# A two-layer hybrid encoder in split float32: 1/rms moved from the tokens to the evictions, and layer 0 started from feature-major tokens

## The chip, the cores and the metric

One core of a Trainium2 chip runs the whole kernel. The metric is the device time of one execution in microseconds; smaller is better. The engines are named as the profile names them: PE (TensorE), PEld (its weight loads), DVE (VectorE), ACT (ScalarE), POOL (GpSimd), SP (SyncE, which here only issues transfers).

## What is computed

512 tokens of 2048 features pass two layers. Per layer, cut to what matters here:

```python
h = rmsnorm(x, g_pre)                       # x * rsqrt(mean(x*x) + EPS) * g_pre
z = h @ w_in                                # columns: GLA q,k,v,gate, low-rank forget gate, attention q,k,v,gate
log_a = log_sigmoid(ga @ w_alpha + b_alpha) / 16
o_gla = rmsnorm(gla_chunk_causal(gq, gk, gv, log_a), g_gla) * silu(gg)
scores = einsum(aq, ak) * D ** -0.5 + rel_bias[clipped distance]     # -inf where masked
o_att = rmsnorm(softmax(scores) @ av, g_att) * silu(ag)
y = concat([o_gla, o_att]) @ w_out
x = x + rmsnorm(y, g_post)
```

`1/rms` is one number a token. A product is linear in its tokens, so the factor can be applied to the tokens before a product or to its result.

## The kernel before, in words

**Precision.** Every float32 operand is split into a high part (a cast on ACT) and a remainder (a subtraction on DVE). A product is three matmuls: high x high, high x low, low x high. Weights come in chunks of 256 rows of a block of 512 columns (512 KB): `raw` or `H` is the chunk, `wh` its high part (L183, ACT), `wl` its remainder (L187, DVE). A token operand `a` is [128, 2 parts, 512]: two slices of 128 features for a half of the tokens (256).

**Blocks.** A layer's input projection has 14 blocks of 512 columns. The first two, the gates of attention, are plain products: `std_gemm` (L283) goes over 8 chunks of features in the order `CO`, for each over its token tiles (128 tokens, four in all), with 6 matmuls a tile and chunk. Each tile has a PSUM bank of its own (four banks for products in all, `ps_mm`, four for other work, `ps_ax`). The very first block is run twice, over token tiles 0 and 1, then 2 and 3, and its weights are loaded and split twice. The other twelve are paired; a pair is one Strassen-like product with seven parts P1 to P7 (`fast_gemm`, L357, or L347 where the result is wanted feature-major). Some operands of these parts are sums of token halves (`token_sums`: S1 to S4, stored to DRAM and read back as `sa`). Results are completed at eviction: a finished sum is kept by `copies` (L314, ACT) and joined with PSUM by `combine` (L319, DVE). The output projection is two plain blocks and one pair (`W23`).

**The start.** `prep_half` prepares half the tokens: load rows (token-major), sum of squares (`square_sum`, L416 on ACT, L417 on DVE), 1/rms by a power on POOL (`rsqrt`, L403), scale the rows (L456, DVE), and for each of 8 chunks four transposes on PE (L466), a scale by the feature gain `gcol` (L476, ACT) and the split (L105 ACT, L106 DVE). In layer 1 the rows come from `finish_token` (the residual sum, L1113, DVE), which also stores them to `x_mid`.

**Users of the products.** Gates go through SiLU (L583) to DRAM. Keys and queries are split per head; queries take the factor -QS, the bias is negated on ACT (L709), and one DVE instruction (L734) adds bias to the scores and gives their minimum, from which ACT takes exp(-x) (L738). The forget gate is a narrow product (L605, 64 matmuls) beside the second block.

**Order.** Engine queues run in order. Main products and side work are interleaved by hand: side work is a list of generators (`tasks`), and `pump` takes some steps after each group of matmuls (`rate`); `until(cond)` takes steps till a condition on the program's own state holds; `drain` takes all. Weight jobs are prepared up to five ahead (`ahead`: loads 5, high parts 4, remainders 3). From the instructions in that order a planner with a cost model makes the order of each engine's queue: what its model sees ready earlier can go earlier. `issue_after` keeps an instruction behind another one on its engine. SP's queue holds the weight loads, the `sa` loads and small loads such as the bias; POOL's holds the stores.

## Time and profile before

| | |
|---|---|
| median of 3 runs | 1702.46 us (1696.93 to 1706.23) |
| profiled execution, span from first to last instruction | 1701.1 us; the page gives no other time of this execution |
| busy: PE / PEld / DVE / ACT / POOL | 1648.9 / 1403.5 / 1209.9 / 873.2 / 160.0 us |
| mean granted clock of PE | 0.991 |
| moved by DMA | 455.04 MB, mean 268 GB/s |

Busy times of engines overlap. A matmul's own length (mean 0.39 us for 512 columns) is longer than the distance at which they follow each other, since they are pipelined. Times in a timeline count from the start of the span; "[1.8 <-X]" behind a row says how long its engine had stood idle and what ended that.

### The profile page before, as it was taken

What the parts mean: (1) busy time and instruction counts of PE and PEld (TensorE: products, weight loads), DVE (VectorE), ACT (ScalarE), POOL (GpSimd) and SP (SyncE); (2) the same over time, 40 slices, a digit from 0 to 9 for tenths busy, and PEclk for the clock granted to TensorE, in tenths of its full rate; (3) what the DMA queues carried; (4) which work ended last, traced back from release to release, by engine and by line L of the source; (5) the groups of instructions that cost most, each with busy time, mean ns of one, the idle gap of its engine ahead of it and who ended that gap; (6) DMA issues with size and microseconds to landing.
All of it is one profiled execution on the core that took longest, in us unless ns stands there. A gap on an engine that the chain in (4) does not pass through costs nothing. (4 is left out here: it accounts for less than half of the span.)

```text
span 1701.1 us, 24915 instructions
## 1 busy us (share of the span) xinstructions
PE 1648.9 (97%) x9090; PEld 1403.5 (83%) x9090; DVE 1209.9 (71%) x1563; ACT 873.2 (51%) x1460; POOL 160.0 (9%) x256
## 2 busy tenths in 40 slices
PE   7999999999999999999999999999999999999995
PEld 5888878999987877787778878799999888777884
DVE  5846867686776876468887567668777667854886
ACT  8634544455665544345684345345556555433443
POOL 0210000001000101210122000000001001022101
PEclk8999999999999999999999999999999999999998
DMA  7986877868858797589779688868587678865993
GB/s 259 364 301 226 331 255 265 281 203 273 294 184 279 242 348 252 175 315 314 251 239 370 240 294 297 290 233 291 192 298 256 210 259 268 300 232 197 354 334 135
DMA packets 143002, 455.04 MB, mean 268 GB/s; under 512 B 15444, under 2 KB 32212, under 8 KB 142880
## 3 DMA queue, kind: packets, MB, share of 16 engines
q1 hardware_dynamic: 119984, 373.76, 64.2%
q0 software_dynamic: 22176, 78.41, 11.9%
q8 instruction: 72, 1.18, 0.3%
q10 hardware_dynamic: 720, 1.28, 0.2%
q14 instruction: 50, 0.41, 0.1%
HBM read 381.28 MB, written 72.11 MB: 267 GB/s over the span
## 5 line engine op out<-in xcount | busy, mean ns | idle before, releaser
L357 PE MATMUL mm<-wh,sa 128*128 128x512 f32 x1536 | 490.3, 394 | 9.1 <-ACT wh L183 4.0
L183 ACT CAST wh<-raw 128x1024 fp32r<-128x1024 f32 x248 | 261.8, 1057 | 276.8 <-PE mm L357 76.4
L187 DVE TENSOR_TENSOR wl<-raw,wh 128x1024 fp32r<-128x1024 f32 x248 | 301.8, 1221 | 96.5 <-PE mm L283 32.2
L357 PEld LDWEIGHTS mm<-wh,sa 128*128 128x128 f32 x1536 | 289.7, 189 | 74.5 <-ACT wh L183 5.8
L183 ACT CAST wh<-H 128x1024 fp32r<-128x1024 f32 x224 | 234.8, 1052 | 225.2 <-PE mm L357 123.9
L187 DVE TENSOR_TENSOR wl<-H,wh 128x1024 fp32r<-128x1024 f32 x224 | 272.3, 1221 | 93.8 <-PE mm L357 33.5
L357 PE MATMUL mm<-wl,sa 128*128 128x512 f32 x768 | 303.2, 395 | 9.5 <-DVE wl L187 9.4
L347 PE MATMUL mm<-sa,wh 128*128 128x256 f32 x1280 | 236.9, 285 | 0.0
L347 PEld LDWEIGHTS mm<-sa,wh 128*128 128x128 f32 x1280 | 200.2, 191 | 0.4
L357 PE MATMUL mm<-wh,a 128*128 128x512 f32 x576 | 184.0, 393 | 2.6 <-DVE t L319 2.6
L347 PE MATMUL mm<-sa,wl 128*128 128x256 f32 x640 | 181.3, 283 | 0.0
L357 PEld LDWEIGHTS mm<-wl,sa 128*128 128x128 f32 x768 | 145.4, 189 | 43.5 <-DVE wl L187 14.5
L283 PE MATMUL mm<-wh,a 128*128 128x512 f32 x512 | 169.4, 395 | 3.6 <-ACT a L105 1.8
L176 DVE TENSOR_TENSOR H<-H,raw 128x1024 f32<-128x1024 f32 x112 | 136.7, 1222 | 1.9
L357 PEld LDWEIGHTS mm<-wh,a 128*128 128x128 f32 x576 | 107.3, 188 | 25.1 <-DVE t L319 3.0
L347 PEld LDWEIGHTS mm<-sa,wl 128*128 128x128 f32 x640 | 122.5, 191 | 0.0
L180 DVE TENSOR_TENSOR raw<-H,raw 128x1024 f32<-128x1024 f32 x48 | 58.8, 1225 | 86.1 <-DMA raw<-in_w_dram 86.0
L403 POOL TENSOR_TENSOR sm<-sm,mhalf 128x2 f32<-128x2 f32 (+2 forms) x44 | 53.2, 1210 | 688.6 <-DVE sm L777 459.9
L283 PEld LDWEIGHTS mm<-wh,a 128*128 128x128 f32 x512 | 95.9, 188 | 26.0 <-ACT a L105 2.3
L357 PE MATMUL mm<-wl,a 128*128 128x512 f32 x288 | 113.5, 394 | 0.9 <-DVE wl L187 0.9
L283 PE MATMUL mm<-wl,a 128*128 128x512 f32 x256 | 100.5, 393 | 0.5 <-DVE wl L187 0.4
L347 PE MATMUL mm<-a,wh 128*128 128x256 f32 x512 | 94.8, 284 | 0.0
(193 smaller groups left out, 2350.9 us busy)
## 6 DMA issues: line engine op xcount, KB each, us to landing
raw<-in_w_dram SPq DMA_DIRECT2D x312, 512.0 KB, 5.2
sa<-S SPq DMA_DIRECT2D x192, 512.0 KB, 5.1
H<-in_w_dram SPq DMA_DIRECT2D x56, 512.0 KB, 4.8
sa<-A SPq DMA_DIRECT2D x48, 512.0 KB, 6.0
S<-g POOLq DMA_DIRECT2D x32, 512.0 KB, 7.8
oS<-g POOLq DMA_DIRECT2D x32, 512.0 KB, 7.1
sa<-oS SPq DMA_DIRECT2D x32, 512.0 KB, 5.5
sg<-t POOLq DMA_DIRECT2D x32, 256.0 KB, 5.5
```

The lines of the kernel that those rows point to most:

```text
L176: nc.vector.tensor_tensor(out=h, in0=h, in1=r, op=ALU.add)
L180: nc.vector.tensor_tensor(out=r, in0=h, in1=r, op=ALU.subtract)
L183: last_cast[0] = nc.scalar.copy(self.wh, src).ins
L187: nc.vector.tensor_tensor(out=self.wl, in0=self.src, in1=self.wh.bitcast(F32), op=ALU.subtract)
L283: nc.tensor.matmul(pss[o], a[:, part, t], rhs[:, kk, :], start=(i == 0 and kk == 0 and m == 0), stop=(i == n - 1 and kk == 1 and m == 2),)
L347: nc.tensor.matmul(dst, lhs[:, kk, f], a[:, part, tok], start=(fresh and kk == 0 and m == 0 and ft % 2 == 0), stop=(c == 3 and kk == 1 and ...
L357: nc.tensor.matmul(out_ps[t], a[:, part, tok], rhs[:, kk, :], start=(fresh and kk == 0 and m == 0), stop=(c == 3 and kk == 1 and m == 2), ...
L403: nc.gpsimd.tensor_tensor(out=out_r, in0=v, in1=mhalf[:, : v.shape[-1]], op=ALU.pow)
```

## The change

Products now take the tokens with only the feature gain applied. 1/rms (and its negative, and rms) of each token is kept in a small tile `norm`, worked out after the operands are prepared (`token_norms`), and also written to DRAM (`r_d`) to be read back as a row across partitions (`norm_row`).

- Evictions multiply by the token's 1/rms: SiLU's scale, `copies`, `combine`, the splits of v, the decay product of k, av. The products of attention's q and k are left as they are: k is multiplied by a row of 1/rms (one more DVE instruction and one small load), and q's factor is applied at the scores, where the bias is first multiplied by rms (one ACT copy a head and tile) and the DVE instruction scales by -1/rms. The bias is no longer negated on load.
- The forget gate's result is multiplied by the row of 1/rms as it leaves PSUM.
- In layer 0 the host gives a second, feature-major copy of the tokens, `xt` (two halves x 8 chunks of 256 KB). Each weight chunk of the first block is loaded between the two halves of its columns; there are no transposes; the gain is applied in place, one 256-wide part on ACT, one on DVE. The rows follow behind the weight chunks 8 to 11, for the squares alone.
- In layer 0 the first block runs once, over all four token tiles.

```diff
 stream: for l in range(L):
-        stream += [Job(l, "std", c, AG0) for c in CO]
-        stream += [Job(l, "std", c, AG0) for c in CO]
+        for _ in range(min(l, 1) + 1):
+            stream += [Job(l, "std", c, AG0) for c in CO]
 Job.load:
-                self.raw = self.fetch(rtile("raw"), b0, c)
+                i = done["load"]
+                if i < NCH:
+                    load_columns(i, 0)
+                    self.raw = self.fetch(rtile("raw"), b0, c)
+                    load_columns(i, 1)
+                else:
+                    self.raw = self.fetch(rtile("raw"), b0, c)
+                if NCH - 1 <= i < NCH + 3:
+                    half, j = divmod(i - NCH + 1, 2)
+                    with tc.issue_after(last_load[0]):
+                        rows[half, j] = load_row(half, j, x, nc.sync)
 copies:
-                nc.scalar.copy(e, src[t])
+                if scaled:
+                    nc.scalar.activation(e, src[t], AF.Copy, scale=inv_rms(l, 2 * (name == "p5") + t))
 combine:
-                nc.vector.tensor_tensor(out=dst, in0=a, in1=b, op=op)
+                if scaled:
+                    r = (inv_rms if sign > 0 else neg_inv_rms)(l, 2 * h + t)
+                    nc.vector.scalar_tensor_tensor(out=dst, in0=ps, scalar=r, in1=kept, op0=ALU.mult, op1=op)
...
+    def token_norms(l, half, xs):
+        cols = slice(2 * half, 2 * half + 2)
+        ss = sm(2)
         for j in range(2):
             square_sum(ss[:, j : j + 1], xs[j])
             yield
+        r = norm[l][:, 0, cols]
         rsqrt(r, ss)
+        nc.vector.tensor_scalar(out=norm[l][:, 1, cols], in0=r, scalar1=-1.0, scalar2=None, op0=ALU.mult)
+        nc.vector.tensor_tensor(out=norm[l][:, 2, cols], in0=ss, in1=r, op=ALU.mult)
         for j in range(2):
-            for z in xs[j]:
-                nc.vector.tensor_scalar(out=z, in0=z, scalar1=r[:, j : j + 1], scalar2=None, op0=ALU.mult)
-            yield
+            t = 2 * half + j
+            nc.gpsimd.dma_start(r_d[l][t * P : (t + 1) * P, :], inv_rms(l, t))
+        normed.add((l, half))
+        yield
+
+    def norm_row(l, tok, n):
+        z = t2((tok.stop - tok.start,))
+        nc.sync.dma_start(z[0:n], r_d[l][tok, :].rearrange("s o -> o s").partition_broadcast(n))
+        return z
 prep_chunk:
+            if l:
+                nc.scalar.activation(d, ps[:, kk * 256 : (kk + 1) * 256], AF.Copy, scale=g)
+            elif kk:
+                nc.vector.tensor_scalar(out=d, in0=d, scalar1=g, scalar2=None, op0=ALU.mult)
+            else:
+                nc.scalar.activation(d, d, AF.Copy, scale=g)
...
+    def prep_half(l, half, xs):
+        for ch in CO:
+            yield from prep_chunk(l, half, ch, xs)
+        yield from token_norms(l, half, xs)
+
+    def prep_first():
+        for i, ch in enumerate(CO):
+            while i not in columns:
+                yield
+            for half in range(2):
+                yield from prep_chunk(0, half, ch, None)
+        for half in range(2):
+            while (half, 1) not in rows:
+                yield
+            yield from token_norms(0, half, [rows[half, j] for j in range(2)])
...
-    xs_first = load_tokens(0, x, nc.sync)
-    prepare("load", 2)
-    xs_second = load_tokens(1, x, nc.sync)
+    prepare("load", 4)
 gate_evac:
-                gate(half, q, o, ps)
+                until(lambda: (l, o // 2) in normed)
+                gate(half, q, o, ps, inv_rms(l, o))
 layer 0, first block:
+            std_gemm(l, AG0, range(NT), CO, operand_in, gate_evac(1, 0), rate=1.0, lag=2)
 Head.scores:
+                nc.scalar.activation(pr, biases[self.hd][:, 512 - lk : 512], AF.Copy, scale=rms(l, i))
                 nc.vector.tensor_tensor_reduce(
-                    out=pr, in0=ps[:, :lk], in1=biases[self.hd][:, 512 - lk : 512], op0=ALU.add, op1=ALU.min,
-                    scale=1.0, scalar=-NEG, accum_out=nmx,
+                    out=pr, in0=ps[:, :lk], in1=pr, op0=ALU.add, op1=ALU.min,
+                    scale=neg_inv_rms(l, i), scalar=-NEG, accum_out=nmx,
 qk_consume, keys:
+                    nc.vector.tensor_tensor(
+                        out=z, in0=z, in1=norm_row(l, hs, P).unsqueeze(1).to_broadcast([P, 2, 256]), op=ALU.mult
+                    )
```

More of the change, by code (lines that the diff above doesn't have):

```diff
@@ L99, in hybrid_trunk @@
     fac_d = [dram([P, 1024], f"fac{l}") for l in range(L)]
+    r_d = [dram([S, 1], f"r{l}") for l in range(L)]
     def flat(t):
@@ L446, in hybrid_trunk, with full_tile, load_columns, inv_rms @@
     full = {}
-    def prep_half(l, half, xs):
-        ss, r = sm(2), sm(2)
+    columns = set()
+    def full_tile(half, c):
+        return rtile("H") if half == 0 else slot(KEEP[c], [2, 512])
+    def load_columns(i, half):
+        kh, c = divmod(CO[i], 4)
+        if kh == 0:
+            full[half, c] = full_tile(half, c)
+        with tc.issue_after(last_load[0]) if last_load[0] else nullcontext():
+            last_load[0] = nc.sync.dma_start(full[half, c][:, kh, :], xt[half, CO[i]]).ins
+        columns.add(i)
+    norm = [small.tile([P, 3, NT], F32, tag="norm", name=nm("norm"), bufs=2) for _ in range(L)]
+    normed = set()
+    def inv_rms(l, t):
+        return norm[l][:, 0, t : t + 1]
+    def neg_inv_rms(l, t):
+        return norm[l][:, 1, t : t + 1]
+    def rms(l, t):
+        return norm[l][:, 2, t : t + 1]
+    def token_norms(l, half, xs):
+        cols = slice(2 * half, 2 * half + 2)
+        ss = sm(2)
         for j in range(2):
@@ L469, in prep_half @@
             if kh == 0:
-                while half == 0 and l and done["low"] < min(h_end + c, len(stream)):
+                h_end = next(i for i, z in enumerate(stream) if z.l == l - 1 and z.b0 == W23[0] and z.kind == "P4")
+                while half == 0 and done["low"] < min(h_end + 1 + c, len(stream)):
                     yield
-                full[half, c] = rtile("H") if half == 0 else slot(KEEP[c], [2, 512])
-            dst = full[half, c][:, kh, :]
-            for kk in range(2):
-                kt = 2 * ch + kk
-                nc.scalar.activation(
-                    dst[:, kk * 256 : (kk + 1) * 256], ps[:, kk * 256 : (kk + 1) * 256], AF.Copy,
-                    scale=gcol[:, base + kt : base + kt + 1],
-                )
@@ L480, in prep_half @@
[L480 to L490 removed]
+                full[half, c] = full_tile(half, c)
+        dst = full[half, c][:, kh, :]
@@ L1149, in w_consume @@
                     pass
-        fast_gemm(l, W23, w_consume, rate=3, end=True, lag=3 if last else 0)
+        fast_gemm(l, W23, w_consume, rate=3, end=True, lag=3 if last else 0, scaled=False)
         for c in range(4):
```

146 lines of the change are left out of this document (87 added, 59 removed).

## The prediction, made before the change was run

> **What bounds the kernel now.** I read the page's head and its slices first, then the stretches in which the slices fall short, then the order of time in those stretches.
>
> ```profile
> span 1701.1 us, 24915 instructions
> PE 1648.9 (97%) x9090; PEld 1403.5 (83%) x9090; DVE 1209.9 (71%) x1563; ACT 873.2 (51%) x1460; POOL 160.0 (9%) x256
> ...
> 0.00:120.11 120.11, 109.50 (x523) 89.81 (x524) 72.61 (x103) 75.34 (x130) 17.73 (x44) 0.96 0.84 312
> 5.20:12.50 7.30, 0.00 (x0) 0.00 (x0) 1.33 (x5) 5.78 (x10) 0.80 (x3) 0.68 1.00 392
> 12.50:18.03 5.53, 5.33 (x25) 4.87 (x25) 4.48 (x7) 4.98 (x11) 0.00 (x0) 0.50 1.04 401
> 18.03:32.00 13.97, 12.14 (x65) 9.66 (x63) 8.68 (x15) 13.97 (x32) 1.23 (x2) 1.00 0.44 161
> 32.00:120.11 88.11, 88.11 (x428) 73.99 (x428) 57.84 (x78) 47.73 (x79) 15.21 (x28) 1.00 0.90 331
> 272.00:460.00 188.00, 188.00 (x1536) 186.19 (x1535) 141.46 (x205) 103.12 (x189) 9.11 (x12) 1.00 0.75 251
> 826.00:890.50 64.50, 58.09 (x275) 46.64 (x274) 54.18 (x76) 54.49 (x107) 16.18 (x29) 0.95 0.67 225
> ```
>
> Columns of the stretches: length, busy time of PE, PEld, DVE, ACT, POOL, granted clock, DMA share, GB/s. TensorE is the bound: 97% busy, and in most stretches without a gap (88.11 of 88.11, 188.00 of 188.00). So only three things move the time: work taken off PE, PE's gaps, and its half clock. Its gaps lie where this change works: in the start (to 120.11, when the first product of the next stage, L357, begins) and at the passage from layer 0 to layer 1 (826 to 890.5, 6.4 us idle and a clock of 0.95). The attention products (272 to 460) have none to give.
>
> The start, in order of time (start, length, engine):
>
> ```profile
> 0.76 0.40 ACTq L534 DMA_DIRECT2D gcol<-in_g_cols_dram  x1
> 4.88 1.06 ACT L416 ACTIVATE t<-g 128x1024 bf16<-128x1024 f32 x1 [1.58 <-DMA g<-in_x_dram]
> 5.84 0.19 ACT L416 ACTIVATION_READ_ACCUMULATOR t<-g 128x1 f32 x1
> 6.54 1.06 ACT L416 ACTIVATE t<-g 128x1024 bf16<-128x1024 f32 x1 [0.51 <-DMA g<-in_x_dram]
> 10.96 0.71 POOL L403 TENSOR_TENSOR sm<-sm,mhalf 128x2 f32<-128x2 f32 x1 [9.94 <-DVE sm L417]
> 11.71 2.74 DVE L456 TENSOR_SCALAR g<-g,sm 128x1024 f32<-128x1024 f32 x4 [0.83 <-POOL sm L403]
> 13.18 5.13 PE L466 MATMUL ax<-cst,g 128*128 128x128 f32 x23 [0.19 <-DVE g L456]
> 18.03 0.52 PE L283 MATMUL mm<-wh,a 128*128 128x512 f32 x1
> 20.44 0.69 ACT L416 ACTIVATE t<-bias 128x512 bf16<-128x512 f32 x1
> 23.73 0.50 PE L283 MATMUL mm<-wh,a 128*128 128x512 f32 x1 [1.76 <-ACT a L105]
> 31.33 0.33 SPq L708 DMA_DIRECT2D bias<-in_rel_dram  x1
> 91.81 2.05 PE L605 MATMUL ax<-g,g 128*96 128x256 f32 x16
> 120.11 0.39 PE L357 MATMUL mm<-wh,a 128*128 128x512 f32 x1
> 1567.15 37.94 PE mm L283 x166
> ```
>
> Tokens land, are squared, rooted on POOL, scaled, transposed, scaled again and split: the first real product is at 18.03, the second group waits for ACT at 23.73, and PE is gapless only from 32. The last row is the price of a 512-wide product in a gapless run: 37.94/166 = 0.2286 us. A forget-gate product is 2.05/16 = 0.128 us, a transpose 5.13/23 = 0.22 at half clock, so 0.11 at full.
>
> **The change, part by part.**
>
> *The start.* Useful PE work before 120.11: 384 products of the first two blocks (192 each, the same number before and after) x 0.2286 = 87.8, and 64 forget-gate products x 0.128 = 8.2: 96.0 us. The rest, 120.1 - 96.0 = 24.1 us, is transposes, idle time and half clock. The change removes the 64 transposes and the chain in front of the first product. What the new first product waits for:
>
> ```profile
> gcol<-in_g_cols_dram ACTq DMA_DIRECT2D x1, 32.0 KB, 4.3
> bias<-in_rel_dram SPq DMA_DIRECT2D x16, 256.0 KB, 4.5
> L183 ACT CAST wh<-raw 128x1024 fp32r<-128x1024 f32 x248 | 261.8, 1057 | 276.8 <-PE mm L357 76.4 <-PE mm L283 50.4 <-DMA raw<-in_w_dram 50.4
> L187 DVE TENSOR_TENSOR wl<-raw,wh 128x1024 fp32r<-128x1024 f32 x248 | 301.8, 1221 | 96.5 <-PE mm L283 32.2 <-PE mm L357 28.0 <-PE mm L347 13.8
> L105 ACT CAST a<-H 128x512 fp32r<-128x512 f32 x16 | 10.0, 675 | 0.0
> L106 DVE TENSOR_TENSOR a<-H,a 128x512 fp32r<-128x512 f32 x16 | 10.7, 687 | 4.8 <-ACT a L105 4.7
> L476 ACT ACTIVATE H<-ax,gcol 128x256 f32<-128x256 f32 x32 | 13.0, 515 | 0.3 <-PE ax L466 0.3
> L709 ACT ACTIVATE bias<-bias 128x512 f32<-128x512 f32 x16 | 10.5, 657 | 18.2 <-DMA bias<-in_rel_dram 18.2
> L456 DVE TENSOR_SCALAR g<-g,sm 128x1024 f32<-128x1024 f32 x12 | 8.6, 750 | 3.2 <-POOL sm L403 3.2
> ```
>
> SP now issues half a chunk of columns (256 KB), the weights (512 KB), the other half. By the rows at 4.88 and 6.54, 512 KB lands at 4.9 and the next 1.66 later, so the columns land near 4.1 and the weights near 5.7 (estimates from those rows). The gains of the features are issued at 0.8 and take 4.3: 5.1, so they come last. Then scale 0.5 (ACT one part, DVE the other) to 5.6, cast 0.68 to 6.3, weight cast 1.06 to 7.35 (the first product), weight remainder 1.22 to 8.6 (the second product, before which PE can't go on). I take 8.6 as the start.
>
> The clock: 0.68 over 5.20 to 12.50 means half clock for 64% of 7.3, that is from 7.8 on, so the first products meet it. Two rows price the way back:
>
> ```profile
> 830.69:834.72 4.03, 4.03 (x10) 2.91 (x10) 3.69 (x5) 2.75 (x5) 1.23 (x3) 0.60 0.96 315
> ```
>
> There a clock of 0.60 over 4.03 us of products is 3.2 us at half speed, 1.6 us lost. At 12.50 to 18.03, 25 matmuls, nearly all transposes, stayed at 0.50 for 5.5 us: 2.8 lost. The new stage begins with products, so I take 1.6 and keep 2.8 as the far end; below stands 0, if the first product comes before 7.8.
>
> The Trainium skill, TensorE: Matmul & The Clock Gate, Part 4, says that transposes don't count as busy for the clock gate, and Part 1 that some 3.4 us of activity release it. The trace agrees so far: 3.2 us of products against 5.5 us of transposes. If the rule did not hold, the far price would go into the sum and the forecast be 1.2 us later.
>
> Supply of the first block: PE needs 24 x 0.2286 = 5.5 us a chunk. ACT has 2 x (0.5 + 0.68) + 1.06 = 3.4, DVE 2 x (0.4 + 0.69) + 1.22 = 3.4 (a 256-wide scale bounded by half of the 0.75 of L456). Into the same eight chunks fall the squares of the four rows, 6 pieces x 1.25 (4.88 with its read at 5.84) and 4 x 0.9 (20.44, with a read) = 11.1 us of ACT: 38.5 of 43.9 us. That is tight, and before, ACT was full (13.97 of 13.97) just where PE waited 1.8 us for it. I put 2.0 us of PE waits here; ends 0 and 4.8 (all gaps and half clock of before between 12.5 and 32: 0.2 + 2.8 + 1.8). The second weight pass goes (8 transfers, 8 casts, 8 remainders); the 4 MB of columns take its place on the queue, and the DMA share of 0.90 stays below one.
>
> Sum: 8.6 + 1.6 + 96.0 + 2.0 = 108.2 against 120.1: **11.9 us** gained. Norms: the rows arrive behind weight chunks 8 to 11, near 40 us by PE's pace of 5.5 us a chunk, and the first eviction is at 10.2 + 156 x 0.2286 = 46; the root is due then, with some 4 us in hand. If late, the next block's first tile still has 3 tiles x 12 products = 8 us before it needs the bank.
>
> *The passage to layer 1.* There the squares, root and scaling leave the way from the residual sum to the transposes:
>
> ```profile
> 868.92 1.41 DVE L1113 SCALAR_TENSOR_TENSOR sg<-g,sm,sg 128x512 f32<-128x512 f32 x2
> 873.95 1.80 POOL L403 TENSOR_TENSOR sm<-sm,mhalf 128x2 f32<-128x2 f32 x1 [2.79 <-DVE sm L417]
> 875.79 1.42 DVE L456 TENSOR_SCALAR g<-g,sm 128x1024 f32<-128x1024 f32 x2 [0.61 <-POOL sm L403]
> 877.35 0.52 PE L466 MATMUL ax<-cst,g 128*128 128x128 f32 x3 [0.36 <-DVE g L456]
> 881.15 0.33 PE L466 MATMUL ax<-cst,g 128*128 128x128 f32 x1 [1.82 <-ACT g L476]
> 884.35 0.78 PE L283 MATMUL mm<-wh,g 128*128 128x512 f32 x1
> ```
>
> Tokens are final at 870.3, transposes start at 877.35: 7 us that the change takes out. The products of the first pass end at 876.8 and those of the second start at 884.35: 7.6 us, of which 32 transposes x 0.11 = 3.5 stay. So at most 4.1 us come back, by the operands' being ready 6 to 7 us sooner. The squares (about 5 us of ACT a half) move behind the preparation, into a stretch where ACT is 54.49 of 64.50 busy; what is late next is ACT's casts, worth some tenths. I take **4.0**; ends 1 and 6 (6.4 idle in the whole stretch; the finishing sums on DVE stay).
>
> *Evictions.* Scaling by a column replaces copies and differences one for one (same shapes, same engines): nothing, PE being covered by 188.00 of 188.00.
>
> *Bias and key rows.* 64 more ACT copies, four a head, of 512, 384, 256 and 128 elements; the first at 0.66, the rest in proportion plus a fixed part, together about 1.8 a head, less one 0.66: +18.7 us on ACT in both layers. 16 key multiplications of 0.69 on DVE: 11 us. Beside 188 us of PE a layer, ACT goes from 103 to 112 and DVE from 141 to 147: hidden. Each multiplication also waits for a small transfer on SP, and behind it on DVE stand the weight remainders:
>
> ```profile
> SPq L166 <- PE mm L347: 99.4, 46, 8.5
> ```
>
> SP waits 2.2 us on average for a buffer (8.5 at worst), and the nearest transfer takes 4.5 (the bias): 6.7 us until it lands. PE then still has two prepared jobs, 24 products each; at 188.00/1536 = 0.122 us that is 5.9. I take 0.12 us of loss each, **2 us** in all; ends 0 and 16 x 0.8 = 13.
>
> *Rest.* One table load fewer, and 8 tiny stores of 1/rms on POOL's queue (beside 160 us of POOL work): nothing.
>
> **Sum:** 1701.1 - 11.9 - 4.0 + 2.0 = 1687.2. The page gives the span alone; the median of the runs shown stands 1.4 above it (1696.93 to 1706.23), so 1688.6, given as **1689 us**, 0.8% faster. About 0.5% (8.5 us) is what a measurement of this kernel can tell from no change.
>
> **Rivals.**
>
> *The start is given back.* ACT (88% by the sum above), or the DMA (312 GB/s x 120 us = 37.5 MB, which at the 331 of the stretch from 32 takes 113 us) paces the first blocks. With the dip of the clock the start ends at 113 + 1.6 and gains 5.5, the rest 2: 1702.5 - 7.5 = 1695, no change by the bound. For it: ACT full at 18 to 32. Against it: 392 to 401 GB/s in the first 18 us, and ACT freed of the second pass.
>
> *Norms come late.* The order of the squares among casts is a planner's; if a row is squared late, eviction waits, and the next block with it: four squares 3.6, the root 0.7 and a cast 1.1 in front, some 6 us lost, 1695 too. For it: the squares of the second half stood ahead of the cast that PE waited for (20.44, 23.73).
>
> *Slower: the key rows.* If SP reaches the row behind its worst wait, 8.5 + 4.5 = 13 us pass, 5.9 are covered, and 7 us x 16 is lost. It decides from (13.9 + 8.5 + 2)/16 = 1.5 us a row; at 2.5 each the time is 1702.5 - 15.9 + 40 = 1727. For it: DVE is one queue. Against it: such small loads go out early when their buffer is free (the bias of the attention stage is issued at 31.33).
>
> *More than forecast.* No half clock, no waits at the start, 6 at the passage: 1702.5 - 15.5 - 6 = 1681.
>
> **Numbers.** Forecast 0.52, more than forecast 0.16, start given back 0.14, late norms 0.09, key rows 0.09. Faster by over 0.5%: 0.52 + 0.16 and a third of the two at 1695, 0.75; the same 0.16; slower 0.09. The range 1679 to 1701 leaves out the key rows and the tails: about 2 in 10. The likeliest case alone spans 1684 to 1694.
>
> **What the profile after would show.** First product of the first block between 7 and 9 us, clock 1.0 from about 12; no transposes before 800; first product of the next stage at 105 to 111. At the passage no wait of transposes for a scaling, and under 3 us between the passes beside the transposes. Attention still gapless; if PE waits for remainders behind a key multiplication, the slow rival holds. The prediction is wrong if the first block's PE waits exceed 5 us or such waits appear 16 times.

## The result, and the profile after

The changed kernel takes 1676.67 us (median of 4 runs, 1676.27 to 1681.29) where the kernel before, run beside it, takes 1702.16 (1696.93 to 1706.23): a ratio of 0.9865, 95% interval 0.9837 to 0.9893. The forecast was 1689, faster by 0.8%; it is faster by 1.35%, and the time lies 2.3 us under the range's lower end. The profiled execution has a span of 1675.1 us (before: 1701.1), so 26.0 us are to be found.

The page's head of the changed kernel, and its stretches in the columns of the prediction (length, busy time of PE, PEld, DVE, ACT, POOL, granted clock, DMA share, GB/s):

```profile
span 1675.1 us, 24838 instructions
PE 1634.3 (98%) x9026; PEld 1393.7 (83%) x9026; DVE 1209.5 (72%) x1575; ACT 884.5 (53%) x1483; POOL 163.1 (10%) x264
```

```profile
0.00:105.79 105.79, 101.47 (x458) 81.90 (x459) 61.96 (x105) 60.77 (x103) 20.29 (x48) 0.98 1.03 342
6.33:50.57 44.24, 43.72 (x191) 35.88 (x192) 30.39 (x53) 31.86 (x57) 5.12 (x11) 1.00 1.09 354
50.57:56.50 5.93, 4.01 (x11) 2.82 (x10) 2.26 (x7) 4.97 (x9) 2.88 (x5) 0.73 0.96 338
259.12:449.98 190.86, 190.86 (x1582) 190.02 (x1580) 146.75 (x216) 112.53 (x216) 9.58 (x12) 1.00 0.76 258
803.33:867.83 64.50, 57.57 (x273) 45.97 (x272) 54.45 (x77) 51.27 (x99) 13.81 (x30) 0.97 0.63 223
```

PE has 64 instructions fewer (the transposes of layer 0) and is 14.6 us less busy; the rest of the 26 us was idle time. The start is 14.3 us shorter (105.79 for 120.11). The attention products were gapless before and are now. The passage (last row) is not better. The row is moved by 22.67 us, so that it starts as long ahead of layer 1's first product (830.35 here, 853.02 before) as the row 826.00:890.50 of the prediction does: 58.09 us busy before, 57.57 now, and two points of clock more.

To see where the rest came from I cut every profile at the first product of each stage. The stage lengths in us, of the kernels of this study (GG/AV is the two pairs of GLA gates and attention values, GK/GV the two pairs of GLA keys, queries and values, W23 the second half of the output projection; "first stage" is layer 1's two plain blocks with the passage in front of their second):

| kernel | next stage at | GG/AV, layers 0, 1 | GK/GV, layers 0, 1 | W23, layer 0 | layer 1's first stage | span |
|---|---|---|---|---|---|---|
| before | 120.11 | 157.23, 156.84 | 190.14, 192.40 | 87.76 | 104.90 | 1701.1 |
| before again | 120.37 | 154.57, 156.41 | 190.34, 193.50 | 86.36 | 103.47 | 1698.0 |
| all subtractions moved | 120.12 | 153.92, 154.09 | 191.93, 191.75 | 86.65 | 103.36 | 1695.6 |
| one subtraction moved | 120.31 | 154.25, 153.89 | 189.89, 190.94 | 86.79 | 103.85 | 1691.6 |
| token-major start | 117.33 | 154.50, 155.42 | 187.87, 188.45 | 85.80 | 109.61 | 1691.9 |
| changed | 105.79 | 153.33, 154.72 | 188.80, 188.30 | 84.70 | 107.98 | 1675.1 |
| changed again | 108.39 | 153.39, 154.57 | 189.43, 189.49 | 83.92 | 109.19 | 1679.8 |
| without 1/rms | 101.92 | 154.76, 153.88 | 193.28, 195.01 | 83.86 | 99.86 | 1675.3 |
| early rows | 104.43 | 158.53, 154.88 | 187.68, 188.99 | 83.92 | 113.24 | 1682.0 |
| corner left out | 103.92 | 154.23, 153.50 | 189.00, 189.00 | 84.00 | 113.39 | 1678.4 |
| norms behind both halves | 105.72 | 153.56, 155.08 | 188.97, 188.41 | 83.78 | 111.53 | 1680.7 |
| corner and norms | 103.26 | 154.41, 153.53 | 188.21, 189.91 | 83.99 | 107.24 | 1672.3 |
| all three | 102.87 | 155.72, 154.37 | 189.15, 188.47 | 84.04 | 104.48 | 1671.3 |
| all three again | 111.47 | 156.07, 153.88 | 189.05, 189.46 | 84.05 | 107.06 | 1681.7 |

(The attention stages, 190.8 to 192.1, and the first half of the output, 106.9, are left out: they hardly differ.) From before to changed: start 14.3, GG/AV 3.9 and 2.1, GK/GV 1.3 and 4.1, W23 3.1, layer 1's first stage -3.1, attention and end 0.2: by these rounded terms 25.8 of the 26.0 us. So the passage as a whole (W23 and first stage) gave nothing where 4.0 were forecast, and 11.4 us came from stages that the forecast put at nothing.

One pair of profiles is not enough for such a sum. From "before again" to "changed again" it reads: start 12.0, GG/AV 1.2 and 1.8, GK/GV 0.9 and 4.0, W23 2.4, first stage -5.7. And the 6.0 us of GG/AV in the first pair can't be put down to the change: the kernel with one subtraction moved (below) has the kernel before's queues everywhere but in GK/GV, and its GG/AV took 154.25 and 153.89, as in the changed kernel. The first profile of the kernel before was long there.

**The start.** Rows of the changed kernel:

```profile
3.73 0.51 ACT L542 ACTIVATE H<-H,gcol 128x256 f32<-128x256 f32 x1 [1.73 <-DMA gcol<-in_g_cols_dram]
5.23 1.04 ACT L197 CAST wh<-raw 128x1024 fp32r<-128x1024 f32 x1 [0.34 <-DMA raw<-in_w_dram]
6.33 0.73 PE L297 MATMUL mm<-wh,a 128*128 128x512 f32 x2 [0.70 <-ACT wh L197]
7.59 0.50 PE L297 MATMUL mm<-wl,a 128*128 128x512 f32 x1 [0.52 <-DVE wl L201]
...
35.24 1.61 SPq L458 DMA_DIRECT2D sg<-in_x_dram  x2
47.11 0.63 ACT L439 ACTIVATE t<-sg 128x512 bf16<-128x512 f32 x1 [2.18 <-DMA sg<-in_x_dram]
51.53 0.63 ACT L439 ACTIVATE t<-sg 128x512 bf16<-128x512 f32 x1 [3.70 <-DMA sg<-in_x_dram]
52.16 1.25 ACT L660 ACTIVATE t<-mm,norm 128x512 f32<-128x512 f32 x2
52.88 0.50 PE L297 MATMUL mm<-wh,a 128*128 128x512 f32 x1 [1.92 <-ACT t L660]
```

The chain in front of the first product is the one forecast, only quicker: the gains are there at 3.7. But for the 0.52 us at 7.59, products then run without a gap to 50.57. There they need a bank that tile 0's eviction (L660) is to free, and on ACT's queue the squares of the last row's pieces stand ahead of it: issued at 35.24, landed at 47.1 and 51.5. PE stands 1.92 us, and the clock of the stretch is 0.73.

**Layer 1's first stage.** Rows of DVE and PE in the changed kernel:

```profile
885.75 0.11 DVE L798 MEMSET bias<- 64x64 f32 x1 [6.81 <-DMA bias<-in_rel_dram]
885.85 1.23 DVE L201 TENSOR_TENSOR wl<-raw,wh 128x1024 fp32r<-128x1024 f32 x1
887.13 0.50 PE L297 MATMUL mm<-wl,sa 128*128 128x512 f32 x1 [2.37 <-DVE wl L201]
```

The memset that writes the masked corner of a bias tile has to follow the tile's transfer. Before, ACT's negation of the bias waited for that transfer (18.2 us of its idle time in the prediction's row of L709) and the memset came behind the negation. The change drops the negation; now the memset waits for the transfer itself, and it stands early in DVE's queue, in front of a weight remainder that PE needs. The Trainium skill, PSUM — Partial Sum Buffer, section "Engine vs sequencer instructions", says that ACT's, DVE's and POOL's queues are strictly first in, first out; the trace agrees: the remainder starts 0.1 us after a memset that stood 6.81 us.

### The profile page after: what moved, and what is told of

Same layout as the page of the kernel before. It is cut to its first block, busy times and chain, and to the rows that moved or that the text cites. A ratio compares the mean times of both kernels' runs of the same rounds, so it can differ in the third digit from the quotient of the medians.

```text
span 1675.1 us, 24838 instructions
## 1 busy us (share of the span) xinstructions
PE 1634.3 (98%) x9026; PEld 1393.7 (83%) x9026; DVE 1209.5 (72%) x1575; ACT 884.5 (53%) x1483; POOL 163.1 (10%) x264
## 4 chain that ended last, share of the span: by engine, by line
PE 81%; DMA 8%; DVE 5%; ACT 3%; issue 2%; POOL 0%; DVEq 0%; SPq 0%; ACTq 0%; POOLq 0%
PE mm L380 39%; PE mm L370 16%; PE mm L297 16%; DMA raw<-in_w_dram 4%; PE ax L856 2%; DVE wl L201 2%; PE ax L380 1%; PE ax L1018 1%; DMA sa<-S 1%; PE ax L1052 1%; PE ax L839 1%; DMA sg<-in_x_dram 1%; DMA bias<-in_rel_dram 1%; ACT wh L197 1%; PE ax L687 1%
## 5 line engine op out<-in xcount | busy, mean ns | idle before, releaser
L197 ACT CAST wh<-raw 128x1024 fp32r<-128x1024 f32 x240 | 252.3, 1054 | 274.6 <-PE mm L380 87.5
L201 DVE TENSOR_TENSOR wl<-raw,wh 128x1024 fp32r<-128x1024 f32 x240 | 292.2, 1220 | 102.6 <-PE mm L297 43.8
L426 POOL TENSOR_TENSOR sm<-sm,mhalf 128x4 f32<-128x4 f32 (+2 forms) x40 | 48.0, 1201 | 667.4 <-DVE sm L866 444.8
L194 DVE TENSOR_TENSOR raw<-H,raw 128x1024 f32<-128x1024 f32 x48 | 58.8, 1225 | 70.1 <-DMA raw<-in_w_dram 70.1
```

The source lines that it names most:

```text
L194: nc.vector.tensor_tensor(out=r, in0=h, in1=r, op=ALU.subtract)
L197: last_cast[0] = nc.scalar.copy(self.wh, src).ins
L201: nc.vector.tensor_tensor(out=self.wl, in0=self.src, in1=self.wh.bitcast(F32), op=ALU.subtract)
L426: nc.gpsimd.tensor_tensor(out=out_r, in0=v, in1=mhalf[:, : v.shape[-1]], op=ALU.pow)
```

## The experiments

**Repeats of both kernels.** What does a kernel differ from itself by?

> The kernel before, profiled a second time, for its four stages of paired products with token-major results (first profile: 157.2, 190.1, 156.8 and 192.4 us, together 696.6; in the changed kernel 685.2). Theory 'landing': the difference of 11.5 us is made by when weights land, which differs from run to run, so the sum here moves by 3 us or more from 696.6. Theory 'order': it is made by the changed evictions and the queue orders that follow from them, so the sum here is 696.6 within 1.5 us.

> The changed kernel once more, beside the others on one chip. Theory 'order' (the stages' gains are set by the order of the queues): start 99 to 100 us, GK/GV 188 to 189 us in both layers, layer 1's first stage 108 us with VectorE's stand of 7 us at the bias. Rival 'chance': layer 1's first stage and the first attention stage differ by 3 us or more from 108.0 and 153.3. Whole 1675 to 1679, ratio 0.985 to 0.989.

The kernel before once more: 1699.77 us in one run. The changed kernel once more: 1675.0 us (1672.68 to 1681.55, 6 runs), ratio 0.9873 (0.985 to 0.9895). The table shows what holds in both pairs: GK/GV 188.3 to 189.5 against 190.1 to 193.5, the start, the longer first stage of layer 1. The 3.9 us of GG/AV in layer 0 do not: the kernel before had 154.57 the second time. Its four stages sum to 694.8, 1.8 under the first time: "order" allowed 1.5, "landing" asked for 3. Of the changed kernel's repeat, layer 1's first stage (109.19) and GG/AV are as "order" had them, GK/GV a little over, but the start is not 99 to 100 us long, it is 102.1. So the start moved by 2.6 us by itself:

```profile
50.36 0.63 ACT L439 ACTIVATE t<-sg 128x512 bf16<-128x512 f32 x1 [4.97 <-DMA sg<-in_x_dram]
53.05 0.63 ACT L439 ACTIVATE t<-sg 128x512 bf16<-128x512 f32 x1 [1.97 <-DMA sg<-in_x_dram]
53.68 0.67 ACT L660 ACTIVATE t<-mm,norm 128x512 f32<-128x512 f32 x1
```

The same row of tokens, issued at the same time, landed 1.5 us later, and eviction and products with it. The rest of the 2.6 is half clock: 0.66 over the 9.93 us from 50.57, which is 6.8 us at half speed, for 3.2 the first time (0.73 over 5.93).

**The start undone.** The changed kernel with layer 0 prepared as before:

```diff
-        for _ in range(min(l, 1) + 1):
+        for _ in range(2):
             stream += [Job(l, "std", c, AG0) for c in CO]
...
-    tasks.append(prep_first())
+    tasks.append(prep_half(0, 0, xs_first))
+    tasks.append(prep_half(0, 1, xs_second))
```

> The changed kernel with layer 0 started as before: token-major rows, transposes, the first block in two passes; 1/rms at the evictions stays. No squares, root or scaling stand before the transposes, so the first product comes near 13 us (18.0 before, 6.3 in the changed kernel) and the next stage starts near 116 (120.1 and 105.8). Theory 'landing': the pair stages add up to anything between 685 and 697, the total is near 1685 to 1695. Theory 'order': the pair stages keep the changed kernel's 685 but for the first (its order on VectorE is here that of before, 2.6 us), total near 1688.

It takes 1690.85 us (1687.71 to 1693.65), ratio 0.9952 (0.9935 to 0.9969). So 1/rms at the evictions is worth 0.5%, about 8 us, without the feature-major start. Some 3 of these come at the start (117.33 for 120.11), where squares, root and scaling no longer stand in front of the transposes; the first product came at 16.43 and not near 13, since transposes waited for the constants and for ACT. GK/GV is short here too (187.87, 188.45), and the four stages sum to 686.2, near what "order" had, though "landing" allowed that too. So the gain of GK/GV belongs to the evictions and not to an earlier start. The feature-major start is worth the rest, 0.8% or some 13 to 15 us.

**No 1/rms at all.** This kernel leaves out every factor of 1/rms and the squares, and keeps the negated bias of the kernel before:

```diff
-        yield from token_norms(l, half, xs)
-                gate(half, q, o, ps, inv_rms(l, o))
+                gate(half, q, o, ps, 1.0)
-            nc.vector.memset(b[0:64, 448:512], MASKED)
+            nc.scalar.activation(b, b, AF.Copy, scale=-1.0)
+            nc.vector.memset(b[0:64, 448:512], -NEG)
```

> The changed kernel with the whole of 1/rms left out (no rows, squares, roots, scalings, key rows; evictions as before; the tokens stay un-normalised): the feature-major start alone, and the price of all that handles 1/rms as the difference. The wait of 2.3 us at 50 us with its half clock goes (4 us), and of the passage's waits those behind squares and behind the bias fill (some 5 us). Theory 'order': its queue orders in the pair stages are those of before, so these take 696 again and the total is near 1677. Theory 'landing': the pair stages take 685 to 697 by chance, total 1665 to 1677.

It takes 1676.28 us (1672.21 to 1679.69): no less than the changed kernel, with less to do. What the norms cost is gone (start 101.92 for 105.79, layer 1's first stage 99.86 for 107.98), but GK/GV is at 193.28 and 195.01. The four stages sum to 696.9 and the whole is near 1677, as "order" had both. That pointed to the queues: in this kernel DVE's weight operations stand in the order of the kernel before, in the changed kernel and in the token-major one GK/GV has another.

**All subtractions moved.** In every pair of the input projection, four chunks need `H` minus `raw` (L180 before, L194 after), which waits for the weight's transfer. Where this stands in front of a remainder `wl` whose inputs are there, it holds up the remainder. So, in the kernel before:

```diff
+                    with tc.issue_after(last_low[0]):
                         nc.vector.tensor_tensor(out=r, in0=h, in1=r, op=ALU.subtract)
```

> The kernel before with one addition: on VectorE the subtraction that completes a weight part's rounded copy (raw minus the rounded part) is kept behind the last remainder wl issued before it; nothing else of the change is in it. Theory 'order' (the change gains in the attention stages of the values and the gate because VectorE no longer stands at a subtraction that waits for the weight's landing while a remainder whose inputs are ready is queued behind it): the two GK/GV stages come down from 190 to 195 us to 187 to 189.5 each, the four attention stages together from 695 to 697 to about 686 to 690, and the whole to about 1692 (1687 to 1696, ratio 0.993 to 0.998). Rival 'landing' (these stages differ by when the weight's transfers happen to land, or by the eviction itself): GK/GV stays at 190 to 195, the whole at 1697 to 1703, ratio 0.998 to 1.002. Both: start and layer 1's first stage as before (first product at 18, 102 and 104 us long).

It takes 1698.51 us, ratio 1.0007 (0.9993 to 1.0021). The theory's number failed: GK/GV 191.93 and 191.75. The wait it was aimed at did go (no wait of PE for `sa` there any more), and PE's idle time in layer 0's stage fell from 3.8 to 3.2 us; but its busy time rose from 186.3 to 188.7. The edit did more than it was meant to: the planner wrote out the queues of PE and ACT in another order too. 36 narrow products of GLA, before in groups of up to 12 and here in groups of up to 6 between wide ones, took longer in sum (before, then this run):

```profile
L921 PE MATMUL ax<-g,g 64*128 64x256 f32 x36 | 3.7, 312 | 0.0
L923 PE MATMUL ax<-g,g 64*128 64x256 f32 x36 | 4.9, 317 | 0.0
```

A second kind of them went from 2.2 to 2.8 us: together 1.8 us, as much as the stage grew (190.14 to 191.93). So this run says nothing against the theory; it is no test of it.

**One subtraction moved.** Among the subtractions of these two pairs, one stands at another place in DVE's queue in the changed kernel than before: the first of the pair GV0/GV1. (Two places a layer also differ where weight parts are added; they were not tested.) This run moves that one instruction a layer, in the kernel before, to where the changed kernel has it:

```diff
+                    if (self.b0, c) == (GV0, 0):
+                        with tc.issue_after(p["low", 1]):
                             nc.vector.tensor_tensor(out=r, in0=h, in1=r, op=ALU.subtract)
```

> The kernel before with one instruction moved in each layer: on VectorE the first subtraction raw minus high of the pair GV0/GV1 is kept behind the remainder of the second weight part of the product before it (the place that it has in the changed kernel); all else of VectorE's, ScalarE's and SyncE's order is as before. Theory 'order at this place': SyncE's weight load behind that remainder then waits about 2 us in place of 5.6, the load of sa behind it on SyncE's queue comes about 3 us earlier, TensorE's wait 140 us into the stage of GK, GQ and GV falls from 1.9 to 3.0 us to under 1.2 and the half clock behind it goes; the two stages come to 188 to 189.5 us (190.1 to 193.5 before), the whole is 3 to 6 us shorter: ratio 0.9965 to 0.998. Rival 'elsewhere' (as the run with all subtractions reordered, which had no wait there and stages of 191.8 to 191.9 us all the same): the wait goes and another takes its place; the stages stay at 190 us or more, ratio 0.999 to 1.001.

It takes 1693.69 us (1691.11 to 1695.84, 12 runs) against 1699.68, ratio 0.997 (0.9955 to 0.9985): one instruction a layer is worth about 5 us. What it changes in layer 1, in order of time, is this. The kernel before:

```profile
1436.74 1.23 DVE L180 TENSOR_TENSOR raw<-H,raw 128x1024 f32<-128x1024 f32 x1 [4.04 <-DMA raw<-in_w_dram]
1438.22 1.22 DVE L187 TENSOR_TENSOR wl<-raw,wh 128x1024 fp32r<-128x1024 f32 x1
1439.50 0.33 SPq L141 DMA_DIRECT2D raw<-in_w_dram  x1
1439.92 1.21 SPq L166 DMA_DIRECT2D sa<-S  x2
```

One subtraction moved:

```profile
1428.51 1.22 DVE L191 TENSOR_TENSOR wl<-raw,wh 128x1024 fp32r<-128x1024 f32 x1
1429.79 0.33 SPq L141 DMA_DIRECT2D raw<-in_w_dram  x1
1431.09 1.23 DVE L182 TENSOR_TENSOR raw<-H,raw 128x1024 f32<-128x1024 f32 x1 [1.36 <-DMA raw<-in_w_dram]
1433.66 0.85 SPq L166 DMA_DIRECT2D sa<-S  x2
```

PE's wait for `sa` (total, times, longest) and the stretch from 122 us into the stage, in the kernel before,

```profile
PE mm L357 <- DMA sa<-S: 2.6, 1, 2.6
1427.63:1457.63 30.00, 27.44 (x116) 22.25 (x115) 17.55 (x20) 11.65 (x15) 1.68 (x3) 0.94 0.94 315
```

with one subtraction moved,

```profile
PE mm L363 <- DMA sa<-S: 0.6, 1, 0.6
1419.63:1449.63 30.00, 29.41 (x132) 24.06 (x131) 20.44 (x24) 14.51 (x19) 3.13 (x4) 1.00 0.94 343
```

and in the changed kernel:

```profile
PE mm L380 <- DMA sa<-S: 0.8, 1, 0.8
1406.67:1436.67 30.00, 29.20 (x131) 23.57 (x130) 20.05 (x21) 15.98 (x20) 1.68 (x3) 1.00 0.96 348
```

The chain runs over three queues. Before, DVE stands 4.04 us at the subtraction. The remainder behind it frees a weight buffer late, and SP, which waits to load into that buffer, sends this weight only at 1439.50, right in front of the tokens `sa`. PE waits 2.6 us for `sa` and then runs at half clock for a while (0.94). With one instruction moved, the remainder goes first, the weight is sent 3.9 us ahead of `sa`, and PE waits 0.6.

Not every step came as expected. `sa` is not sent earlier: counted from the start of the stage it goes out at 134.3 us before and at 136.0 with the instruction moved, so sending it sooner is not what gained. PE also came later to this place in this profile, since six to eight products at half clock followed the gate's transposes near 73 us, and how much of the shorter wait is due to that stays open. The stages came to 189.89 and 190.94, short of the 188 to 189.5 expected. So the 5 us are shown by the time of 12 runs; the profile shows 1.7 us of them in GK/GV against the first profile of the kernel before and 3.0 against the second.

**Early rows.** The rows for layer 0's norms loaded at chunks 3 to 6 in place of 7 to 10:

```diff
-                if NCH - 1 <= i < NCH + 3:
+                if 3 <= i < 7:
```

> The changed kernel with the four token rows loaded behind weight chunks 3 to 6 of the first block instead of 7 to 10. Theory 'late row': at 50.6 us PE waits 2.3 us and then runs 3 us at half clock because the eviction of tile 0 stands on ScalarE behind the squares of the last row, whose pieces land 11 to 15 us after their issue; with the rows early the wait and the half clock go, the second stage starts 3.5 to 4 us sooner (near 102), total near 1671. Rival 'full queue': the DMA is at a share of 1.05 over this stretch, so what the rows no longer wait for, the columns or weights do, and the stage starts at 105 to 106 as now.

It takes 1683.81 us (1675.89 to 1688.68, 5 runs), ratio 0.9912 (0.9881 to 0.9943): no gain; if anything a loss. In its profile the squares are done by 43.6 us, PE's wait for the eviction is 0.8 us for 1.9, and the next stage starts at 104.43, between the two theories; what was lost lies behind the start (GG/AV 158.53, layer 1's first stage 113.24). Nor is PE's wait safely gone. In the run with all three edits, repeated (below), it is 5.1 us, and these rows stand in the place of the squares:

```profile
54.96 1.04 ACT L197 CAST wh<-raw 128x1024 fp32r<-128x1024 f32 x1 [5.51 <-DMA raw<-in_w_dram]
56.95 1.84 ACT L660 ACTIVATE t<-mm,norm 128x512 f32<-128x512 f32 x3
```

Now a weight's cast stands ahead of the eviction in ACT's queue and waits 5.5 us for its transfer. "Late row" was only half the cause: the DMA engines are full in these 50 us (share 1.09 in the changed kernel), and here something else that ACT needs was late. It goes without a wait in some executions: with corner and norms the same row, at the old place, came 3 us sooner than in the changed kernel, and PE was gapless:

```profile
48.34 0.63 ACT L439 ACTIVATE t<-sg 128x512 bf16<-128x512 f32 x1 [1.93 <-DMA sg<-in_x_dram]
48.97 0.67 ACT L660 ACTIVATE t<-mm,norm 128x512 f32<-128x512 f32 x1
```

**The corner left out of the transfer.** The memset then has no transfer to wait for (the tile is `bias`, which attention adds to its scores; the expectation calls it the forget gate's):

```diff
-            nc.sync.dma_start(b, ...)                       # [128, 512]
+            nc.sync.dma_start(b[0:64, 0:448], ...)
+            nc.sync.dma_start(b[64:P, :], ...)
             nc.vector.memset(b[0:64, 448:512], MASKED)
```

> The changed kernel with the forget gate's bias loaded in two transfers that leave out the corner of 64 x 64 which the memset on VectorE then fills, so that the memset waits for no transfer. Theory 'mask' (removing ScalarE's negation put the wait for the bias's transfer on VectorE's queue, in front of remainders that TensorE waits for): VectorE's stand of 6.8 us at the memset goes, TensorE's wait of 2.8 us at a remainder at 884 goes, layer 1's first stage is 104 to 106 us long in place of 108.0, and the whole is 2 to 4 us under the changed kernel: about 1673 (ratio to before 0.982 to 0.986). Rival 'late weights' (the remainders are late because the weight's rounded parts wait for their transfers all the same): the memset's stand goes, but TensorE's wait comes back at another remainder or at a rounded part, the stage stays at 107 to 109 us and the whole within 1 us of the changed kernel, about 1676.

**Layer 1's norms behind both halves,** with the forget gate's weights behind them:

```diff
-                yield from prep_half(l + 1, pair, xs)
-                if pair == 0:
+                for ch in CO:
+                    yield from prep_chunk(l + 1, pair, ch, xs)
+                if pair == 1:
+                    for half, z in ((0, xs0), (1, xs)):
+                        yield from token_norms(l + 1, half, z)
```

> The changed kernel with layer 1's 1/rms computed behind the preparation of both halves of the tokens instead of behind each half. Theory 'full queue' (TensorE's waits of 1.1 and 1.6 us at 838 and 840 and the half clock up to 845 come from the squares and the forget gate's splits that stand in ScalarE's and VectorE's queues ahead of the weight's parts of the first products): both waits and most of the half clock go, layer 1's first stage is about 103 to 104 us in place of 108.0, and the whole about 1672.5 (ratio to before 0.981 to 0.986). Rival 'late for the eviction' (1/rms then comes too late for the first evictions): the waits at 838 to 845 go, but the wait at the first evictions or transposes grows from 2.5 us to 5 or more; the stage stays at 107 to 110 us and the whole at 1675 to 1679.

**Both, with early rows.**

> The changed kernel with three edits together: the rows for layer 0's 1/rms loaded earlier (as in the run with early rows), the bias's corner left out of its transfer, and layer 1's 1/rms behind both halves. If the three are separate and the pair stage behind the start differs only by chance: next stage at 104.4 (1.4 us gained), layer 1's first stage at 102 to 104 us (4 to 6 us gained), together about 1670 (1666 to 1673, ratio to before 0.979 to 0.983). If early rows really cost in the stages behind them (as the run with early rows alone had 4 us more in the first attention stage and 5 more in layer 1's first stage): about 1675 to 1678, with the first attention stage again at 157 to 159 us.

The corner alone: 1673.58 us (1672.2 to 1680.24), ratio 0.9875 (0.9852 to 0.9898). The norms alone: 1680.93, ratio 0.9908 (0.9888 to 0.9927). All three: 1678.24 (1673.08 to 1682.79), ratio 0.9894 (0.9867 to 0.992). None is told apart from the changed kernel by its time. In the first profiles of layer 1's first stage, though, each edit alone made it longer (113.39 and 111.53 for 107.98) and both together shorter (104.48). PE's waits there show what stands in the way. The corner alone:

```profile
PE ax L525 <- ACT g L538: 3.5, 1, 3.5
PE mm L297 <- DVE wl L201: 3.1, 2, 1.9
PE mm L297 <- ACT wh L197: 2.2, 2, 1.5
```

the norms alone, where the memset stood directly in front of the remainder that PE needed:

```profile
PE mm L297 <- DVE wl L201: 9.0, 1, 9.0
```

(in order of time, DVE:)

```profile
876.70 0.11 DVE L798 MEMSET bias<- 64x64 f32 x1 [5.55 <-DMA bias<-in_rel_dram]
876.79 1.23 DVE L201 TENSOR_TENSOR wl<-raw,wh 128x1024 fp32r<-128x1024 f32 x1
```

And both without early rows (the run below, which differs from the norms alone by the corner only):

```profile
PE mm L297 <- ACT wh L197: 4.6, 2, 2.5
PE mm L297 <- DVE wl L201: 0.5, 1, 0.5
```

With the norms late and the memset waiting for its transfer, PE loses 9.0 us at one remainder; with the norms late and the memset free, 0.5. The stage is shorter by 4.3 us only (111.53 to 107.24), since PE then waits longer for weights' high parts (4.6 us; 2.0 with the norms alone). That is the price of a memset that waits for a transfer in front of work that PE needs, in this order of the queue. With the norms alone the waits near 839 and 841 us went, as "full queue" said; this new one took their place. With the corner alone the stand goes, as "mask" said, but PE's waits come back at other remainders and at high parts, as "late weights" said; at 113.39 the stage was longer than either theory had it. All three together missed their forecast of 1666 to 1673.

**Once more, without early rows, and all three again.**

> The changed kernel with the bias's corner left out of its transfer and layer 1's 1/rms behind both halves, with the rows of layer 0 where the changed kernel has them. Theory 'both or none' (each edit alone left the other's wait: 113.4 us with the corner alone, 111.5 us with the norms alone, 104.5 us with both and early rows): layer 1's first stage is 103.5 to 105.5 us long, TensorE has no wait over 3 us in it, VectorE none for the bias; the start is as in the changed kernel (next stage at 104 to 106 us), the whole about 1673 (ratio to before 0.983 to 0.987). Rival 'chance' (that stage varies by 5 us with the landings of the weights, and 104.5 was a lucky one): 107 to 113 us again, the whole at 1676 to 1680.

> The changed kernel with the three edits (early rows, the bias's corner, layer 1's 1/rms behind both halves) once more. If its first profile (1671.3 us, next stage at 102.9, layer 1's first stage 104.5) is what it does: 1671 to 1676, ratio 0.983 to 0.987, 2 to 4 us under the changed kernel beside it. If its median of 1678 was: no gain over the changed kernel, ratio 0.988 to 0.990, with the time lost in the attention stages.

Corner and norms: 1674.32 us (1671.65 to 1679.07, 5 runs), ratio 0.9872 (0.9847 to 0.9896), the changed kernel beside it 0.9873. All three again: 1678.41 (1673.49 to 1683.46), ratio 0.9889 (0.9865 to 0.9913). Layer 1's first stage is 107.24 and 107.06: between the two theories, with a wait of 2.5 and 1.7 us for a weight's high part 51 us into it. "Both or none" held for the memset and not for the stage's length. No version here is shown to beat the changed kernel.

## Why the prediction was right or wrong, point by point

**The start, forecast 11.9, measured 14.3 and 12.0** (105.79 and 108.39; before, 120.11 and 120.37). The mechanism was right; four terms were off and partly cancel.

- First products: forecast 7.35 and 8.6, measured 6.33 and 7.59. The step that failed is the gains' landing, put at 5.1 from the 4.3 that their one transfer took before; they were there at 3.7.
- The dip of the clock, forecast 1.6: zero. The granted clock is 1.00 over the 44 us from 6.33, so the products came before the time, 7.8, from which the kernel before ran at half clock. But this was luck, and the condition in the prediction ("if the first product comes before 7.8") was too simple. With the corner left out the first product came at 6.71, with all three again at 6.37, and both started at half clock (row below the list), as did the norms alone (7.22; 0.55 over 6 us). The far price of 2.8, which would have held if transposes counted as busy, could not be tested in the changed kernel: there are none left here.
- Waits for supply, forecast 2.0: 0.52 to 50.57 (43.72 of 44.24 busy). ACT kept up at 31.86 of 44.24.
- Norms, forecast nothing, "some 4 us in hand". Wrong in its landing time: the last row was put near 40 us and landed at 51.5, 53.0 and 48.3 in three profiles with the same loads (changed, changed again, corner and norms). Behind it stands the sentence that "the DMA share of 0.90 stays below one": it was 1.09. The stretch 50.57 to 56.50 has 11 products, 2.5 us of work, in 5.93: 3.4 us lost. By the terms: 6.33 + 96.0 + 0.5 + 3.4 = 106.2, against 105.79.

The start at half clock, with the corner left out:

```profile
6.71:12.71 6.00, 5.47 (x16) 4.04 (x17) 5.49 (x10) 5.01 (x10) 0.00 (x0) 0.72 1.04 407
```

A clock of 0.72 over 6 us is 3.4 us at half speed, 1.7 lost: what the forecast had put in.

On the landing of the last row the Trainium skill, SBUF — State Buffer, section "The DMA setup-cost knee", fits a transfer at 2 us and its bytes over 436 GB/s: 2.6 us for a piece of 256 KB, an estimate from that page's fit. Here, with the DMA share at 1.09, two pieces issued from 35.24 took 12 and 15 us (47.11 and 51.53 less the issue times, 35.24 and some 36.5).

**The passage, forecast 4.0, measured 0 and, by the repeats, -3.3.** The transposes no longer wait for 1/rms, as forecast, and W23 is 3.1 us shorter (2.4 by the repeats). The step that failed is "what is late next is ACT's casts, worth some tenths". In layer 1's first stage PE idled 2.7 us before and 6.6 in the changed kernel: 2.4 at the remainder behind the memset of the bias (9.0 with the norms moved), 2.2 where transposes wait for ACT's scaling by the gain (1.8 before), 0.7 and 1.2 near 839 and 841. Without any 1/rms, and with the memset behind ACT's negation as before, the stage is 99.86 and only a wait of 1.2 is left.

**The bias, "hidden", ACT's added copies and all.** Their time is hidden, 190.86 us gapless. But the removed negation was costed as work and not as a wait: it had kept the wait for the bias's transfer on ACT's queue.

**Key rows, forecast -2.0: nothing.** DVE's waits for them in the changed kernel (total, times, longest):

```profile
DVE t L943 <- DMA t<-r: 9.7, 9, 1.9
```

The far case of 6.7 us a row never came, and layer 0's attention stage is 190.86 us long for 190.88 before. Layer 1's is 191.62 for 190.87, less than the kernel before moves by itself (192.09 the second time).

**Evictions and the rest, forecast nothing: the largest miss.** One for one in shape and engine, as forecast, but they changed the order in which DVE's queue was written out, and one subtraction's place is worth 0.30% (0.15 to 0.45), about 5 us. That is shown by the run that moves it alone, and GK/GV is 4.9 to 5.4 us shorter in both pairs of profiles. The other 6.0 of the 11.4 us lie in GG/AV and are not shown to come from the change. That the time came within 2.3 us of the range is therefore not to the credit of the sum: the 4.0 of the passage did not come, and more than twice as much came from terms put at nothing.

**The rivals.** "The start is given back" did not come: products were gapless to 50.57 at 354 GB/s. "Norms come late" came in part, 3.4 us of its 6, and a different amount in each execution. The slow key rows did not come. "More than forecast" had the sum nearest to the time (1681), but not its reasons: no half clock and hardly a wait at the first products was right in the changed kernel (the clock by luck), 6 us at the passage was not.

## What to carry to other kernels

An instruction that is removed may have been the one that did the waiting: ask who waits for that transfer now, and what stands behind it on its queue. A change of equal cost, one for one, can still reorder an engine's queue; compare the queues of both kernels, of all engines, and look for an operation that waits for a transfer ahead of one whose result frees a buffer. Where the transfers are at their limit, a load moved earlier can make another late. And a stage that differs between two profiles of one kernel is no gain of a change: take a second profile of both before adding up stages.

## What the runs showed of the hardware

Short stands can be enough to lose the clock. In the changed kernel two waits of PE, 1.4 us apart, of 0.70 and 1.20 us, were followed by products at half clock, and so was the single one of 1.92 us at 50.57:

```profile
839.43 0.73 PE L297 MATMUL mm<-wh,a 128*128 128x512 f32 x2 [0.70 <-ACT wh L197]
841.37 0.50 PE L297 MATMUL mm<-wl,a 128*128 128x512 f32 x1 [1.20 <-DVE wl L201]
838.00:846.00 8.00, 6.09 (x19) 4.25 (x18) 7.61 (x14) 7.35 (x13) 2.68 (x6) 0.79 0.11 28
```

The Trainium skill, TensorE: Matmul & The Clock Gate, section "Why this matters for your kernels", says to leave no idle gaps over about 3 us between bursts of products. Here gaps under 2 us cost the clock as well: 0.73 over 5.93 us and 0.79 over 8. But not each does. The stand of 2.37 us at 887.13 in the changed kernel was followed by products at full clock, and so was the same pair of stands, 0.67 and 1.20 us, in the run with the corner left out:

```profile
883.00:891.00 8.00, 5.63 (x25) 4.35 (x24) 5.21 (x8) 3.74 (x5) 0.53 (x1) 1.00 0.90 262
836.52:844.52 8.00, 6.13 (x26) 4.45 (x25) 7.61 (x14) 7.35 (x13) 2.68 (x6) 1.00 0.30 47
```

What decides between them no run here shows. In a forecast such a loss is a chance and not a term.
